# Stick-breaking attention: the last group's first eight row blocks in the order 4, 0, 5, 1, 6, 2, 7, 3

## The chip, the core and the metric

The kernel runs on one core of a Trainium2 chip, as one launch. The metric is the device time in microseconds (us); lower is better. The engines are TensorE (PE, with its weight loads as PEld), VectorE (DVE), ScalarE (ACT), GpSimd (POOL) and SyncE (SP), whose queue issues almost all DMA transfers.

## The reference

One transformer layer on x of 2048 x 1024, float32. A combined projection feeds four differential-attention heads and eight stick-breaking heads; their outputs pass through w_out and are added to x, and a SwiGLU feed-forward part follows. The change is in the stick-breaking part, which is strictly causal and works row block by row block:

```python
z = jnp.einsum('bqhd,bkhd->bhqk', qb, k).astype(jnp.float32) * scale
mask = (k_pos[None, :] < q_pos[:, None])[None, None]
log_1mb = jnp.where(mask, jax.nn.log_sigmoid(-z), 0.0)
rem = lax.cumsum(log_1mb, axis=3, reverse=True) - log_1mb
a = jnp.where(mask, jnp.exp(jax.nn.log_sigmoid(z) + rem), 0.0)
return jnp.einsum('bhqk,bkhd->bqhd', a.astype(v.dtype), v)
```

Each of 16 blocks of 128 queries (a row block) needs the keys of all blocks up to its own, so row block i has i + 1 blocks of keys.

## The kernel before

**Stages.** Matmuls run on 16-bit pairs: every float32 operand is split into a high and a low float16 half. The work goes through eight head groups: groups 0 to 3 are one differential head each, groups 4 to 7 are two stick-breaking heads each. Group by group, the 16 input tiles (128 rows each) are projected, and the attention of a group runs while the next group's tiles are projected. In the last group (7) there is no next group: beside its attention run the rest of its own projection, the loading and splitting of w_out (four quarters, `load_wo`) and, from the second half on, the output projection (`out_proj`, line 814) of rows that all groups have finished. The feed-forward part follows.

**A projected tile** (`proj_tile`, 24 matmuls, L325) is copied out of PSUM and split on ScalarE and VectorE (`proj_out`, L360 to L363). The projection has two PSUM tiles (`pj`, named `osc` or `po` when the weight scales and the output projection use them). After four tiles `proj_batch` turns q and k: two transposing DMAs on SyncE's queue (L409), then two copies of q between partition halves (L411). Row blocks 4j to 4j + 3 need tiles 4j to 4j + 3 and the keys of all tiles before.

**Attention of a row block** (`sb_attn`, line 595). `stage_a(i, m, b)` handles row block i, head m of the two, and a piece b of up to 1024 keys. Per 512 keys TensorE makes the scores (L506, and L508 for the mask) in one of four PSUM tiles `sc`; ScalarE takes two sigmoids (L618, L619); VectorE scans the product of (1 - beta) (L621) and multiplies by beta (L622). Row blocks 0 to 7 have a piece of (i + 1) x 128 keys for each head: VectorE's work grows with i. The piece is then split into halves (`split_t`: L89 on ScalarE, L98 on GpSimd) and turned by a DMA (L460, tile `aT`). `stage_b` makes the values (`pv`, L517) `lag` pieces later (five in the last group). In the last group two row blocks i and i + 1 share a PSUM tile `yp`, and after the second one `finish` normalises, turns and stores them (L475 to L496).

**The order.** The loop at line 647 takes the row blocks 0 to 15 in turn. It yields the share of the group's work that is done, by which the driver (lines 862 to 868) calls for projected tiles, and sets `G["fin"]`, up to which row the output projection may go. The order on each engine is then made by a scheduler when the program is built; on the chip each engine's queue runs in that order.

Of the kernel before, what the change touches and what calls it, by code (L numbers as in the profile page):

```python
# [22 lines left out]
NT, KT, NC = S // P, D // P, S // 512  # L23
# [7 lines left out]
NG = 8  # L31
# [3 lines left out]
LAG0, LAG, PF, CD, CS, LO = 0, 8, 8, 1.0, 1.0, 0.5  # L35
# [24 lines left out]
def block(tc, a, out):  # L60
# [3 lines left out]
    with top:  # L64
# [8 lines left out]
        def note(e, ns):  # L73
            load[e] += ns * KW[e]
# [25 lines left out]
        def pri(k):  # L100
            def deco(f):
                @functools.wraps(f)
                def g(*args):
                    with tc.high_priority(PRI[k]) if PRI[k] else nullcontext():
                        return f(*args)
                return g
            return deco

        def nm(s):
            uid[0] += 1  # L110
            return f"{s}{uid[0]}"
# [144 lines left out]
        with ExitStack() as ph1:  # L256
# [6 lines left out]
            def z4():  # L263
                return zp.tile([P, 1028], F32, tag="z4", bufs=ZB, name=nm("z4"))
# [64 lines left out]
            def turned(g):  # L329
                return 4 <= g < NG - 1  # L330
# [117 lines left out]
            @pri("spl")  # L448
            def split_t(src, n, he="ADP", le="DP", wide=None):
                if wide is not None and wide % 5 in (1, 3):  # L450
                    s16 = pp.tile([P, 4, 256], F32, tag="raw", name=nm("s16"))[:].rearrange("p t n -> p (t n)").bitcast(F16)
                else:
                    s16 = s16p.tile([P, 2048], F16, tag="s16", bufs=SB, name=nm("s16"))
                to16(s16[:, :n], src, n, he)
                tt(s16[:, n : 2 * n], src, s16[:, :n], ALU.subtract, n, le)
                if wide is not None and wide % 4 == 3:
                    aT = pp.tile([P, 4, 4, 2, 64], F16, tag="st", name=nm("aT"))[:].rearrange("p c t s e -> p (c t) (s e)")
                else:
                    aT = sp.tile([P, 16, P], F16, tag="aT", bufs=AB, name=nm("aT"))
                SP.dma_start_transpose(aT[:, : 2 * n // P, :], s16[:, : 2 * n])  # L460
                return aT

            @pri("fin")
            def finish(g, G, i, k, yp, ssum=None):
# [30 lines left out]
                note("D", 350 * k + 200)  # L495
                SP.dma_start(ms[i - k + 1 : i + 1, :, g, :].rearrange("i p n -> p i n"), mo[:, :k].rearrange("p i s n -> p i (s n)"))  # L496

            def fq(g, i):
                k = 2 if g == NG - 1 else 4
                return (i % k, k)  # L500

            @pri("sc")
            def score_chunk(G, sc, i, q, m, w, cut=False, turned=False):
                terms = ((m, 0), (2 + m, 0), (m, 1)) if turned else ((2 + m, m), (m, m))
                for o, (a_, b_) in enumerate(terms):
                    last = PE.matmul(sc[:, : 128 * w].rearrange("p (t n) -> p t n", n=P), lhsT=G["q"][i // 4][:, a_, i % 4, :], rhs=G["k"][q][:, b_, 0:w, :], start=o == 0, stop=o == len(terms) - 1)  # L506
                if cut:
                    last = PE.matmul(sc[:, 128 * w - P : 128 * w], lhsT=idb[:], rhs=tri[:], start=False, stop=True, skip_group_check=True)  # L508
                return last.ins

            @pri("pv")
            def pv(G, yp, y0, aT, b, n, o, wd, start, stop):
                nb = n // P
                for j in range(nb):
                    v = G["v"][2 * b + j // 4][:, j % 4, :]
                    for q, (a_, v_) in enumerate(((j, o), (j, o + wd), (nb + j, o))):
                        PE.matmul(yp[:, y0 : y0 + wd], lhsT=aT[:, a_, :], rhs=v[:, v_ : v_ + wd], start=start and j == 0 and q == 0, stop=stop and j == nb - 1 and q == 2, skip_group_check=True)  # L517
# [77 lines left out]
            def sb_attn(g, G):  # L595
                last = {}
                front = []
                wide = [0]
                lag = PD + 2 if g < NG - 2 else PD

                @pri("at")
                def stage_a(i, m, b):
                    L = (i + 1) * 128
                    n = min(1024, L - 1024 * b)
                    be, om = z4(), z4()
                    if b == i // 8:
                        DVE.memset(om[:, n : n + 1], 8192.0)
                    else:
                        DVE.tensor_copy(om[:, n : n + 1], last[m][:, 0:1])
                    last[m] = om  # L610
                    for c in range((n - 1) // 512, -1, -1):
                        lo, hi = 512 * c, min(512 * c + 512, n)
                        w = hi - lo
                        sc = ps.tile([P, 512], F32, tag="sc", bufs=4, name=nm("sc"))
                        front.append(score_chunk(G, sc, i, 2 * b + c, m, w // P, b == i // 8 and hi == n, turned(g)))
                        aside = c == 1 and turned(g)
                        beta = be[:, lo:hi] if aside else sc[:, :w]
                        ACT.activation(om[:, lo:hi], sc[:, :w], AF.Sigmoid, scale=G["nkz"][:])  # L618
                        ACT.activation(beta, sc[:, :w], AF.Sigmoid, scale=G["kz"][:])  # L619
                        ov = om[:, lo:hi][:, ::-1]  # L620
                        DVE.tensor_tensor_scan(ov, ov, sc[:, :w], om[:, hi : hi + 1], op0=ALU.mult, op1=ALU.bypass)  # L621
                        (POOL if aside else DVE).tensor_tensor(be[:, lo:hi], beta, om[:, lo + 1 : hi + 1], ALU.mult)  # L622
                        note("A", 1.7 * w + 400)
                        note("D", 2.1 * w + 150)
                        note("P" if aside else "D", (1.65 if aside else 1.05) * w + 100)
                    wide[0] += 1
                    return n, split_t(be[:, :n], n, "A", "P", wide[0] if g < NG - 2 else None)

                ypd = {}

                def stage_b(i, m, b, n, aT):
                    with tc.issue_after(front[-1]):
                        stage_c(i, m, b, n, aT)

                def stage_c(i, m, b, n, aT):
                    r, k = fq(g, i)
                    if i // k not in ypd:
                        ypd[i // k] = ps.tile([P, 512], F32, tag="yp", name=nm("yp"))
                    yp = ypd[i // k]
                    pv(G, yp, P * r + 64 * m, aT, b, n, 128 * m, 64, r == 0 and m == 0 and b == i // 8, r == k - 1 and m == 1 and b == 0)  # L640
                    if m == 1 and b == 0 and r == k - 1:
                        finish(g, G, i, k, yp)
                        G["fin"] = i + 1

                pend = []
                done = 0
                for i in range(NT):
                    if i % 4 == 0:
                        level()
                    for b in range(i // 8, -1, -1):  # L650
                        for m in range(2):
                            n, aT = stage_a(i, m, b)
                            pend.append((i, m, b, n, aT))
                            if len(pend) > lag:
                                stage_b(*pend.pop(0))
                            done += n // P + CS
                            yield done / (272 + 48 * CS), (i + 1 if b == 0 and m == 1 else i)
                for u in pend:
                    stage_b(*u)

# [117 lines left out]
            def advance(n):  # L778
                while emitted[0] < min(n, NG * NT):
                    next(stream)  # L780
                    emitted[0] += 1
                if emitted[0] == NG * NT and len(wos) < 4:
                    for _ in stream:
                        pass
                    load_wo(3)
# [74 lines left out]
            outs = 0  # L860
            advance(NT - LAG0)
            for g in range(NG):
                advance(NT * g + 4)
                for fr, i in (diff_attn if g < 4 else sb_attn)(g, Gs[g]):
                    advance(max(NT * g + min(4 * (i // 4 + 1), NT), int(NT * (g + 1 + fr) - (LAG * (1 - LF * fr * (g == NG - 1)) if g else LAG0 + (LAG - LAG0) * fr))))
                    while g == NG - 1 and len(wos) == 4 and outs < Gs[g].get("fin", 0) and (outs + 2) * (outs + 3) / 272 < fr - LO:
                        next(op)
                        outs += 1
# [429 lines left out]
```

## Time and profile before

| | |
|---|---|
| median of 3 runs | 2704.64 us (2703.09 to 2706.77) |
| the profiled execution, own time | 2702.93 us |
| its span, first to last instruction | 2701.0 us |
| TensorE busy | 2508.6 us (93%) |
| VectorE busy | 1959.8 us (73%) |
| ScalarE, GpSimd busy | 1344.7 us (50%), 1517.8 us (56%) |

Times in the profile are in us from the first instruction. A row of the order of time has the start, the duration, the engine, the line and operation, output and inputs by the program's names, the shape, the count of like instructions, and in brackets how long the engine was idle before and what ended that. A row of a group has busy time and mean ns of one instruction behind the first bar, and the idle time ahead of them behind the second. A row of stretches has, for each engine, busy time and instructions, then the granted TensorE clock as a share of full speed, the DMA engines' share and GB/s. In a row of waits stand the total in us, the number of waits and the longest.

### The profile page before, as it was taken

Reading aid. Unit: us, or ns where it says so; the run is one execution under the profiler, and the core shown is the slowest. Engines: PE = TensorE matmul, PEld = TensorE weight load, DVE = VectorE, ACT = ScalarE, POOL = GpSimd, SP = SyncE. Lnnn points to the kernel's source line nnn. Section 1 sums busy time; section 2 is a strip of 40 time slices with the busy share of each in tenths; the row PEclk is TensorE's granted clock in tenths of the full one; section 3 lists DMA queues with packets and bytes.
Section 4 is the critical chain, followed back from the end, with each engine's and each line's share of the span. In section 5 each row is a group of like instructions: output and inputs, shape, how many; then the busy total and the mean of one; then the engine's idle time right before and its main releaser. Section 6 shows DMA issues by size and latency. Waiting matters only on the chain. (4 is left out here: it accounts for less than half of the span.)

```text
span 2701.0 us, 50505 instructions
## 1 busy us (share of the span) xinstructions
PE 2508.6 (93%) x19628; PEld 1507.6 (56%) x19628; DVE 1959.8 (73%) x3712; ACT 1344.7 (50%) x2487; POOL 1517.8 (56%) x1097
## 2 busy tenths in 40 slices
PE   7998989899988989889999999999999999999999
PEld 4655656577776776567774444444444444444444
DVE  6898879899989889887866877778685543433434
ACT  4665656567978878765634534435352112111121
POOL 2578767768767767545665755665564332322323
PEclk9999999999999999999999999999999999999999
DMA  6778697768989989997996566565748744635532
GB/s 221 211 163 184 143 200 172 172 145 183 195 175 185 178 166 206 208 205 203 230 317 232 211 232 219 207 239 183 253 171 330 304 159 157 234 132 184 202 110 94
DMA packets 619584, 534.40 MB, mean 198 GB/s; under 512 B 480640, under 2 KB 548224, under 8 KB 609104
## 3 DMA queue, kind: packets, MB, share of 16 engines
q1 hardware_dynamic: 617520, 529.09, 70.1%
q8 instruction: 154, 2.52, 0.4%
q0 software_dynamic: 512, 1.36, 0.2%
q14 instruction: 86, 0.70, 0.1%
q10 hardware_dynamic: 1312, 0.72, 0.1%
HBM read 261.08 MB, written 147.32 MB: 151 GB/s over the span
## 5 line engine op out<-in xcount | busy, mean ns | idle before, releaser
L98 POOL TENSOR_TENSOR s<-z,s 128x1024 f16<-128x1024 f32 (+7 forms) x288 | 471.5, 1646 | 141.8 <-ACT s L89 118.2
L506 PE MATMUL sc<-kT,qT 128*128 128x512 f16 (+3 forms) x1520 | 382.7, 354 | 51.1 <-DVE z L622 18.6
L1104 PE MATMUL pd<-wd,act 128*128 128x512 f16 x1764 | 392.8, 380 | 5.3 <-DVE cu L1038 4.7
L621 DVE TENSOR_TENSOR_SCAN z<-z,sc 128x512 f32<-128x512 f32 (+3 forms) x320 | 352.8, 1112 | 56.5 <-ACT sc L619 34.6
L325 PE MATMUL pj<-w,xt 128*128 128x384 f16 x1920 | 354.6, 333 | 17.1 <-ACT raw L374 5.8
L1004 PEld LDWEIGHTS <-wu 128*128 128x128 f16 x1848 | 181.9, 98 | 224.6 <-issue 12.8
L1004 PEld LDWEIGHTS <-wg 128*128 128x128 f16 x1848 | 181.3, 98 | 222.9 <-issue 9.3
L517 PE MATMUL yp<-v,aT 128*128 128x64 f16 (+1 forms) x4896 | 271.2, 205 | 36.9 <-DMA aT<-s 35.7
L517 PEld LDWEIGHTS <-aT 128*128 128x128 f16 x4896 | 239.1, 100 | 114.4 <-DMA aT<-s 46.7
L98 POOL TENSOR_TENSOR act<-cg,act 128x512 f16<-128x512 f32 x109 | 150.7, 1393 | 259.4 <-ACT act L1063 259.4
L1104 PEld LDWEIGHTS <-act 128*128 128x128 f16 x1764 | 172.9, 98 | 213.5 <-issue 7.2
L325 PEld LDWEIGHTS <-xt 128*128 128x128 f16 x1920 | 187.8, 99 | 147.2 <-issue 23.4
L89 ACT CAST s<-z 128x128 f16<-128x128 f32 (+7 forms) x215 | 173.3, 810 | 135.9 <-DMA aT<-s 44.6
L98 POOL TENSOR_TENSOR stages<-stages 128x512 f32<-128x512 f32 x97 | 171.4, 1767 | 116.5 <-DVE wg L220 42.2
L618 ACT ACTIVATE z<-sc,c 128x512 f32<-128x512 f32 (+3 forms) x320 | 211.2, 665 | 24.4 <-PE sc L506 12.4
L98 POOL TENSOR_TENSOR hs<-hs,cu 128x512 f32<-128x512 f32 x102 | 133.6, 1317 | 159.3 <-DVE hs L1110 59.7
L506 PEld LDWEIGHTS <-qT 128*128 128x128 f16 x1520 | 128.8, 99 | 119.7 <-issue 23.9
L831 PE MATMUL po<-wo,mt 128*128 128x256 f16 x1536 | 182.4, 279 | 12.6 <-DVE xf L834 8.6
L1063 ACT CAST act<-cg 128x512 f16<-128x512 f32 x126 | 76.7, 616 | 231.1 <-DVE cg L1069 192.7
L1110 DVE SCALAR_TENSOR_TENSOR hs<-pd,c,hs 128x512 f32<-128x512 f32 x144 | 106.0, 747 | 115.0 <-PE pd L1104 105.3
L341 PE MATMUL pj<-xt,w 128*128 128x128 f16 x2304 | 177.4, 222 | 6.2 <-DVE v L363 5.2
L1004 PE MATMUL pm<-X,wu 128*128 128x512 f16 x792 | 179.8, 381 | 2.1 <-ACT cg L1049 1.7
(254 smaller groups left out, 4812.3 us busy)
## 6 DMA issues: line engine op xcount, KB each, us to landing
xt<-xs SPq DMA_DIRECT2D x112, 512.0 KB, 4.5
hs<-hd SPq DMA_DIRECT2D x72, 512.0 KB, 4.5
hd<-hs SPq DMA_DIRECT2D x56, 512.0 KB, 5.9
split<-wg SPq DMA_DIRECT2D x11, 1792.0 KB, 6.9
split<-wu SPq DMA_DIRECT2D x11, 1792.0 KB, 6.7
split<-wd SPq DMA_DIRECT2D x11, 1792.0 KB, 6.8
wg<-split SPq DMA_DIRECT2D x11, 1792.0 KB, 7.5
wd<-split SPq DMA_DIRECT2D x11, 1792.0 KB, 9.0
```

The source lines that it names most:

```text
L89: ACT.copy(dst, src)
L98: (DVE if e == "D" else POOL).tensor_tensor(dst, a_, b_, op)
L325: PE.matmul(pj[:, :384], lhsT=xv[:, xi, kt, :], rhs=G["w"][:, wi, kt, :], start=n == 0, stop=n == 23)
L341: PE.matmul(o, lhsT=x_ if c == 2 else w_, rhs=w_ if c == 2 else x_, start=n == 0, stop=n == 23)
L506: last = PE.matmul(sc[:, : 128 * w].rearrange("p (t n) -> p t n", n=P), lhsT=G["q"][i // 4][:, a_, i % 4, :], rhs=G["k"][q][:, b_, 0:w, :] ...
L517: PE.matmul(yp[:, y0 : y0 + wd], lhsT=aT[:, a_, :], rhs=v[:, v_ : v_ + wd], start=start and j == 0 and q == 0, stop=stop and j == nb - 1 a ...
L618: ACT.activation(om[:, lo:hi], sc[:, :w], AF.Sigmoid, scale=G["nkz"][:])
L621: DVE.tensor_tensor_scan(ov, ov, sc[:, :w], om[:, hi : hi + 1], op0=ALU.mult, op1=ALU.bypass)
L831: PE.matmul(po[:, sl], lhsT=mt[:, kt, P * xi : P * xi + P], rhs=wos[2 * h + n][wi][:, kt, :], start=q == 0, stop=q == 23)
L1004: PE.matmul(ps_[:].rearrange("p (t n) -> p t n", n=P), lhsT=wv[:, wo, wi, 128 * kt : 128 * kt + 128], rhs=X[xo][:, :, xi, kt, :], start=st ...
L1104: PE.matmul(po[:], lhsT=act[:, ao, xi, 128 * j : 128 * j + 128], rhs=W["d"][:, wo, wi, :], start=start and u == 0 and q == 0, stop=u == nu ...
L1110: DVE.scalar_tensor_tensor(dst, po[:], kd[:], src, op0=ALU.mult, op1=ALU.add)
```

## The change

In the last group the first eight row blocks are taken in the order 4, 0, 5, 1, 6, 2, 7, 3; row blocks 8 to 15 and all other groups stay as they were. The bookkeeping follows: a pair of row blocks is finished when its second one is (4 and 5 first, then 0 and 1), `G["fin"]` becomes the first row block that has not ended, and the tiles asked of the projection are those of the highest row block up to the next one.

```diff
+            def row_order(g):
+                pairs = [i for j in range(4) for i in (4 + j, j)]
+                return (pairs if g == NG - 1 else list(range(8))) + list(range(8, NT))
...
                     if m == 1 and b == 0 and r == k - 1:
                         finish(g, G, i, k, yp)
-                        G["fin"] = i + 1
+                        ended.update(range(i - k + 1, i + 1))
+                        G["fin"] = next(t for t in range(NT + 1) if t not in ended)
 
                 pend = []
                 done = 0
-                for i in range(NT):
-                    if i % 4 == 0:
+                ended = set()
+                order = row_order(g)
+                for at, i in enumerate(order):
+                    if at % 4 == 0:
                         level()
...
-                            yield done / (272 + 48 * CS), (i + 1 if b == 0 and m == 1 else i)
+                            yield done / (272 + 48 * CS), (max(order[: at + 2]) if b == 0 and m == 1 else max(order[: at + 1]))
...
-                advance(NT * g + 4)
+                advance(NT * g + 4 * (row_order(g)[0] // 4 + 1))
```

The same instructions stand on each engine in both kernels (one copy of a projected tile moves from VectorE to ScalarE). Their order differs from the place of row block 0's first score on to about row block 12, and in a few swaps at the start of the feed-forward part.

SyncE's queue before, from the last transposes of group 6 on (the first two rows). `aT` of sizes 2, 4, 6 and 8 are row blocks 0, 1, 2 and 3, `aT` of size 10 row block 4; `qT_17777` and `kT_17778` are tiles 4 to 7:

```order
L460 DMA_TRANSPOSE aT_17675<-s_17672 128x16x128
L460 DMA_TRANSPOSE aT_17720<-s_17717 128x16x128
L460 DMA_TRANSPOSE aT_17960<-s_17957 128x2x128
L423 DMA xt_18194<-xs 128x2048
L460 DMA_TRANSPOSE aT_17976<-s_17973 128x2x128
L460 DMA_TRANSPOSE aT_17992<-s_17989 128x4x128
L460 DMA_TRANSPOSE aT_18008<-s_18005 128x4x128
L409 DMA_TRANSPOSE qT_17777<-st_17338 128x8x128
L460 DMA_TRANSPOSE aT_18057<-s_18054 128x6x128
L460 DMA_TRANSPOSE aT_18073<-s_18070 128x6x128
L409 DMA_TRANSPOSE kT_17778<-st_17338 128x8x128
L460 DMA_TRANSPOSE aT_18093<-s_18090 128x8x128
```

The same place on SyncE's queue in the changed kernel (the four `xt` are the inputs of tiles 10 to 13):

```order
L460 DMA_TRANSPOSE aT_17675<-s_17672 128x16x128
L460 DMA_TRANSPOSE aT_17720<-s_17717 128x16x128
L409 DMA_TRANSPOSE qT_17777<-st_17338 128x8x128
L409 DMA_TRANSPOSE kT_17778<-st_17338 128x8x128
L411 DMA qT_17777<-qT_17777 64x1024 x2
L423 DMA xt_18150<-xs 128x2048
L423 DMA xt_18286<-xs 128x2048
L423 DMA xt_18364<-xs 128x2048
L423 DMA xt_18467<-xs 128x2048
L496 DMA ms<-mo_17942 128x4x256
L460 DMA_TRANSPOSE aT_17967<-s_17964 128x10x128
L460 DMA_TRANSPOSE aT_17990<-s_17987 128x10x128
```

The turning of tiles 4 to 7 has moved ahead of every transpose of the group's row blocks, and the first of these is now row block 4's.

ScalarE before, around row block 8's first sigmoid (`z_18717<-sc_18719`). `pj_18474` and `pj_18544` are tiles 13 and 14:

```order
L360 ACTIVATE st_18393<-pj_18474 128x4x64
L89 CAST s_18629<-z_18611 128x1024
L360 ACTIVATE v_18392<-pj_18544 128x2x64
L360 ACTIVATE st_18393<-pj_18544 128x4x64
L618 ACTIVATE z_18717<-sc_18719,c_15239 128x128
L619 ACTIVATE sc_18719<-sc_18719,c_15238 128x128
```

ScalarE in the changed kernel, from row block 3's last sigmoids (`sc_18721`) to row block 8's first (`sc_18747`). `pj_18656` is tile 15, and L189 squares the last quarter of w_out for its scale:

```order
L622 ACTIVATE z_18719<-sc_18721,c_15239 128x512
L623 ACTIVATE sc_18721<-sc_18721,c_15238 128x512
L360 ACTIVATE v_18366<-pj_18656 128x2x64
L189 ACTIVATE wo_18691,m_18701<-z_18692 128x1024
L622 ACTIVATE z_18745<-sc_18747,c_15239 128x128
L623 ACTIVATE sc_18747<-sc_18747,c_15238 128x128
L360 ACTIVATE st_18367<-pj_18656 128x4x64
L189 ACTIVATE wo_18691,m_18701<-z_18693 128x1024
```

Tile 15's first copy and one square have moved ahead of row block 8's first sigmoid. (The changed kernel's line numbers are higher by 4 to 7 behind the new function.)

## The prediction

> **What bounds the kernel now.** I read the page first, then a table of stretches around the changed rows, then TensorE's waits there, then the order of time on each engine.
>
> ```profile
> PE 2508.6 (93%) x19628; PEld 1507.6 (56%) x19628; DVE 1959.8 (73%) x3712; ACT 1344.7 (50%) x2487; POOL 1517.8 (56%) x1097
> core 0: us, PE busy (x) PEld busy (x) DVE busy (x) ACT busy (x) POOL busy (x), PEclk, DMA share, GB/s
> 1086.00:1112.00 26.00, 21.78 (x268) 14.61 (x266) 24.60 (x48) 17.39 (x36) 18.96 (x14) 1.00 0.92 215
> 1112.00:1125.00 13.00, 9.97 (x68) 6.25 (x69) 6.80 (x17) 4.40 (x11) 5.37 (x5) 0.98 0.85 161
> 1125.00:1159.00 34.00, 26.83 (x222) 16.45 (x221) 32.42 (x61) 27.14 (x55) 16.20 (x11) 0.86 0.93 216
> 1159.00:1178.00 19.00, 14.87 (x181) 9.86 (x180) 12.28 (x27) 13.84 (x32) 5.91 (x5) 0.94 1.00 253
> 1178.00:1241.00 63.00, 58.12 (x590) 48.50 (x588) 47.85 (x81) 34.54 (x61) 36.58 (x29) 0.96 0.74 180
> ```
>
> Over the whole span TensorE is the bound. Around the change it isn't. The eight row blocks run from 1086 to 1159, in two halves. Row blocks 0 to 3 end with a lull (1112 to 1125: VectorE busy 6.80 of 13). Row blocks 4 to 7 are VectorE's stage (32.42 of 34.0, 95%). Then a second lull (1159 to 1178: VectorE 12.28 of 19) before row block 8 and the first out-projection. From 1178 TensorE is busy 58.12 of 63, so a lead on TensorE there is a lead of the kernel. In the first four stretches (92 us) TensorE is idle 18.6 us: the most that a better order could find.
>
> ```profile
> PE sc L506 <- DVE z L622: 5.1, 7, 2.1
> PE pj L325 <- DVE st L363: 3.5, 3, 1.9
> PE sc L506 <- DMA qT<-qT: 2.7, 1, 2.7
> ```
>
> These are TensorE's largest waits from 1086 to 1178: on scans, on copies that free the projection's two PSUM tiles, and once on the turned q of tiles 4 to 7, which row block 4 needs.
>
> **The change part by part.** It removes and adds no work. It takes row block 4 first, so nothing of the eight can start until tiles 4 to 7 are projected and turned.
>
> *Row block 4 starts earlier, 0 to 3 later.*
>
> ```profile
> 1088.41 4.07 PE L325 MATMUL pj<-w,xt 128*128 128x384 f16 x24
> 1094.36 0.97 PE L325 MATMUL pj<-w,xt 128*128 128x384 f16 x5
> 1097.72 1.95 PE L325 MATMUL pj<-w,xt 128*128 128x384 f16 x11 [0.46 <-DVE st L363]
> 1103.26 4.23 PE L325 MATMUL pj<-w,xt 128*128 128x384 f16 x25
> 1107.32 1.65 PE L517 MATMUL yp<-v,aT 128*128 128x64 f16 x51
> 1124.25 0.22 PE L506 MATMUL sc<-kT,qT 128*128 128x128 f16 x1 [2.69 <-DMA qT<-qT]
> 1097.15 0.42 DVE L363 SCALAR_TENSOR_TENSOR st<-pj,st 128x256 f16<-128x256 f32 x1
> 1112.57 1.26 SPq L409 DMA_TRANSPOSE qT<-st  x1
> 1116.57 1.31 SPq L409 DMA_TRANSPOSE kT<-st  x1
> 1121.15 1.20 SPq L411 DMA_DIRECT2D qT<-qT  x2
> ```
>
> With the scores of rows 0 to 3 gone from this place, TensorE ends tile 6 at about 1093 and has nothing until tile 5's copy frees a PSUM tile. That copy ends at 1097.57 now, and some 0.5 earlier without row 0's scan and product ahead of it: tile 7 starts at 1097.1, after 4.1 us of idle. Ahead of row 4's first score then stand three tiles of 24 matmuls (0.163 each by the 4.07 row: 3.9 a tile), 96 value matmuls of row block 15 (51 took 1.65: 2.8), and 0.5 for a weight scale: 15.0 us. The clock adds something: both halved stretches below follow idle time.
>
> ```profile
> 1124.50:1134.70 10.20, 7.50 (x57) 4.41 (x55) 9.09 (x18) 9.59 (x22) 3.82 (x3) 0.50 0.91 302
> 1175.70:1182.50 6.80, 5.97 (x30) 3.91 (x30) 3.71 (x15) 5.56 (x12) 6.47 (x5) 0.50 0.74 169
> ```
>
> In the second, half of 5.97 busy us was lost, 3.0; so the gap costs 0 to 3.0, and I take 1.7. Row 4's scores come at 1097.1 + 15.0 + 1.7 = 1114, against 1124.25. The turns don't bind: before, four transposes of rows 2 and 3 stood among those of tiles 4 to 7 on SyncE's queue; now the three issues follow each other from about 1106, and the copies' 3.1 us (1121.15 to 1124.25) end near 1113. Behind them on SyncE the loads of tiles 10 to 13 stand ahead of row 4's first transpose, and the last of these must wait for tile 10's matmuls, about 1121 (1114, row 4's 1.6 of scores, 3.9, and 1.5 of other matmuls between). Row 4's halves are split at about that time too, and five later pieces run before its values are wanted: I cost this at 0, and 1 us if that cover is gone.
>
> On a gap like this one the Trainium skill ("TensorE: Matmul & The Clock Gate", "HAM oscillation — how this bites in real kernels") warns of idle gaps over about 3.4 us. The trace is stricter: the clock halved at 1124.5 behind a wait of 2.69, and at 1175.7 behind waits of at most 1.47. By the page only the new 4.1-us gap would be punished and the sum stays at -4; by the trace short gaps ahead of the out-projection can be too, and it would be about -1.
>
> *One run of eight row blocks instead of two halves.*
>
> ```profile
> L621 DVE TENSOR_TENSOR_SCAN z<-z,sc 128x512 f32<-128x512 f32 x10 | 12.7, 1274 | 0.4 <-ACT sc L619 0.3
> L622 DVE TENSOR_TENSOR z<-sc,z 128x512 f32<-128x512 f32 x10 | 6.8, 681 | 0.2
> L621 DVE TENSOR_TENSOR_SCAN z<-z,sc 128x384 f32<-128x384 f32 x2 | 2.0, 1002 | 0.0
> L621 DVE TENSOR_TENSOR_SCAN z<-z,sc 128x256 f32<-128x256 f32 x2 | 1.5, 728 | 0.0
> L622 DVE TENSOR_TENSOR z<-sc,z 128x384 f32<-128x384 f32 x2 | 1.1, 552 | 0.1
> L621 DVE TENSOR_TENSOR_SCAN z<-z,sc 128x128 f32<-128x128 f32 x2 | 0.9, 474 | 2.7 <-ACT sc L619 2.7
> L622 DVE TENSOR_TENSOR z<-sc,z 128x256 f32<-128x256 f32 x2 | 0.8, 418 | 0.0
> L622 DVE TENSOR_TENSOR z<-sc,z 128x128 f32<-128x128 f32 x2 | 0.6, 284 | 0.0
> 1125.19 0.48 DVE L621 TENSOR_TENSOR_SCAN z<-z,sc 128x128 f32<-128x128 f32 x1 [2.66 <-ACT sc L619]
> 1158.70 0.06 DVE L607 MEMSET z<- 128x1 f32 x1
> 1165.33 0.48 DVE L621 TENSOR_TENSOR_SCAN z<-z,sc 128x128 f32<-128x128 f32 x1 [2.47 <-ACT sc L619]
> ```
>
> Scan and product cost 0.76, 1.15, 1.55 and 1.96 for blocks of 128 to 512, twice (two heads) a row: rows 0 to 3 are 2 x 5.42 = 10.8 us. Before, that lay in the time in which tiles 4 to 7 were waited for; now it stands in the run. Rows 4 to 7 took 33.5 (1125.19 to 1158.70). Add 10.8, and 2.0 for a few copies (0.42 each) and the end of group 6's last output that fall into the run now: 46.3. From row 4's first scan (1114 + 0.9) the run would end at 1161.2. What I charge beyond that are two places in ScalarE's order.
>
> ```profile
> 1124.60 1.25 SPq L802 DMA_DIRECT2D z<-in_w_out_dram  x2
> 1132.96 1.05 ACT L189 ACTIVATE wo<-z 128x1024 bf16<-128x1024 f32 x1
> 1164.70 0.37 ACT L618 ACTIVATE z<-sc,c 128x128 f32<-128x128 f32 x1 [2.29 <-PE sc L506]
> ```
>
> First, the square of the third quarter of w_out. It ran 8.4 us after its loads were issued. The loads now come behind three transposes of rows 4 and 0, at about 1127, so the square comes near 1135.5, while row 6's sigmoids, which stand behind it, could run at about 1133.5: 2 us. Second, tile 15's copy and another square now stand ahead of row 8's first sigmoid (before, only tile 14's copies did). From row 3's last score TensorE has tiles 14 and 15 (7.8), some 105 value matmuls (3.1) and row 8's own scores (1.0, and a short wait for a free tile): about 13 us. VectorE has about 10.5 left there. With the square (1.05) this costs 4 us. Row 8's first scan comes at 1161.2 + 2 + 4 = 1167 to 1168, against 1165.33: VectorE is 2.5 late.
>
> *The out-projection starts earlier.*
>
> ```profile
> 1174.68 0.60 PE L506 MATMUL sc<-kT,qT 128*128 128x512 f16 x2 [1.47 <-DVE z L607]
> 1177.84 6.48 PE L831 MATMUL po<-wo,mt 128*128 128x256 f16 x37
> 1241.01 0.28 PE L506 MATMUL sc<-kT,qT 128*128 128x128 f16 x2
> ```
>
> Its first matmul stood behind row block 9's first scores, which wait for scans (1.47 at 1174.68). Now it stands behind row 8's only and the last weight scale, whose second square follows row 8's first sigmoid by about 2 us: 1170. Some 3.3 us of scores and values that were done before it now come later. TensorE's lead is 1177.84 - 1170 - 3.3 = 4.5. To row block 12's first score (1241.01) it has about the same matmuls left in both kernels and is busy 92% of the time, so the lead holds; for VectorE's 2.5 I take off 0.5. From there the engines' orders agree, but for a few swaps where the feed-forward part starts, which I cost at 0 (1 either way).
>
> **Sum:** -4 us. The profiled execution took 2702.93 (span 2701.0 and 1.9 around it), so 2698.9 of it; the median of the runs is 2704.64, 1.7 above, so I say 2700.6.
>
> **Rivals.** A measurement of this kernel can tell about 0.2% (5.4 us) from no change.
>
> *VectorE is late and passes it on (slower).* In the mixed run large and small blocks alternate, and VectorE waits for ScalarE at small ones: the 128 blocks' rows show 2.7 us of idle before two scans, the 512 blocks' 0.4 before ten. Against it: the 2.7 is row 4's start. If VectorE packs the run to 80% instead of 95%, 46.3 becomes 55, row 8's scan comes at about 1176, and the first out-projection at 1178.5: with the 3.3 that is +4 on TensorE, and with VectorE 11 late the scores between the out-projection's matmuls make TensorE wait: +8, 2712.6. It decides from row 8's first scan at about 1171.
>
> *The lulls really go (clearly faster).* No wait in ScalarE's order: row 8 at 1161.2, the out-projection at 1164, and the halved stretch at 1175.7 (3.0) gone with the waits ahead of it. TensorE's lead would be 1177.84 - 1164 - 3.3 = 10.5; I give 9, since VectorE would be only 4 early: 2695.6. For it speaks that TensorE is no obstacle beside the run (26.83 of 34.0 busy); against it stand the two places in ScalarE's order. That the change doesn't reach the engines at all is out: their order shows it.
>
> **How the numbers follow.** Forecast 0.48 (-8 to 0 around -4), clearly faster 0.20, slower 0.32. Of the forecast three tenths lie beyond -5.4, of the slower case three quarters beyond +5.4. Faster: 0.48 x 0.3 + 0.19 = 0.33; slower 0.24, say 0.25; the rest, 0.42, within 0.2%. The range of 8 in 10 takes most of both rivals: 2691 to 2712.
>
> **What would show it.** Row 4's first score near 1114 behind one TensorE gap of about 4 us; VectorE above 90% busy from there to row 3's scans; row 8's first scan at 1165 to 1169; the first out-projection by 1171; row block 12's first score near 1237. A first scan of row 8 behind 1171, or an out-projection that starts early and then waits for its PSUM tiles, would prove me wrong.

## The result and the profile after

The changed kernel is slower: its median is 2713.36 us (17 runs, 2706.53 to 2729.47) against 2705.57 (17 runs, 2700.83 to 2712.96) for the kernel before on the same chip, a ratio of 1.0031 with a 95% interval of 1.0018 to 1.0044. That is 8.4 us more (4.9 to 11.9), where 4 less were forecast, and outside the range.

The page of the changed kernel, its span and the engines' busy time:

```profile
span 2711.4 us, 50503 instructions
...
PE 2503.5 (92%) x19628; PEld 1502.0 (55%) x19628; DVE 1960.6 (72%) x3711; ACT 1345.0 (50%) x2488; POOL 1517.3 (56%) x1097
```

The span is 10.4 us longer and TensorE is busy 5.1 us less: over the whole program all the loss is idle time. The stretches that the prediction used, for the changed kernel:

```profile
core 0: us, PE busy (x) PEld busy (x) DVE busy (x) ACT busy (x) POOL busy (x), PEclk, DMA share, GB/s
1086.00:1112.00 26.00, 21.73 (x207) 13.85 (x206) 17.20 (x33) 7.36 (x15) 14.68 (x9) 0.93 1.06 237
1112.00:1125.00 13.00, 8.17 (x63) 4.90 (x62) 11.46 (x27) 11.30 (x28) 3.52 (x4) 0.87 0.68 161
1125.00:1159.00 34.00, 30.02 (x269) 18.87 (x268) 30.49 (x63) 27.78 (x57) 20.22 (x16) 0.95 0.81 200
1159.00:1178.00 19.00, 12.89 (x136) 8.99 (x135) 9.62 (x25) 9.41 (x24) 5.12 (x6) 0.82 0.99 231
1178.00:1241.00 63.00, 52.46 (x542) 42.77 (x541) 49.84 (x82) 38.47 (x68) 35.00 (x26) 0.95 0.72 177
```

VectorE's lull of 1112 to 1125 is gone (11.46 of 13 busy, 6.80 before). But TensorE's idle time of the first four stretches is 19.2 us (92 less 72.81), not less than the 18.6 of before: it only lies elsewhere. And from 1178 to 1241, where TensorE was to keep its lead, it is busy 52.46 of 63 instead of 58.12.

To see where the time goes over the whole program, each TensorE instruction was matched with the same one in the profile of before; the table has the median difference of their starts in four stretches (us, times of before; positive is later):

| | 1000-1080, ahead of the change | 1390-1440, behind the attention | 1640-1720, in the feed-forward part | 2400-2680, near the end |
|---|---|---|---|---|
| changed kernel | -2.6 | 2.9 | 9.9 | 10.3 |
| changed kernel, profiled again | -0.2 | 2.3 | 9.3 | 9.0 |

So there are two steps. The attention moves by +5.5 in one execution and +2.5 in the other; the start of the feed-forward part adds 7.0 in both. Behind it nothing more is lost. The prediction had -4 and 0 for them. The 7.0 stands out from the spread of single executions; the attention's step hardly does: five kernels of the experiments below, whose attention is that of before, have steps from -0.1 to +4.0 there, 2.4 on average.

**The start of the feed-forward part.** Each kernel's TensorE waits from 1440 to 1560, of before and then of after (`xtr` are transposes of the rows that have just been normalised, `pa` the first products of the feed-forward part):

```profile
PE xtr L1178 <- DVE bx L228: 3.4, 2, 3.1
...
PE pa L1004 <- ACT cg L1014: 1.7, 1, 1.7
```

```profile
PE xtr L1185 <- DVE bx L228: 7.8, 2, 6.9
PE pa L1011 <- ACT cg L1021: 4.1, 2, 2.4
```

These two waits have grown most, by 4.4 and 2.4 us. They are not the whole of the 7.0: the same matmuls take 235.06 us before (1425.13 to 1660.19) and 242.00 after (1428.00 to 1670.00), in which TensorE is busy 215.75 and 218.65 at a mean granted clock of 0.98 and 0.96. So its idle time grows by 4.0, since other waits became shorter, and its busy time by 2.9. Both waits lead back to ScalarE, but to two places in its queue. The first place: ScalarE's order of time before, with the row of SyncE that loads row 14 (`bx`, the second of two such loads; the longer of their two landings took 9.7 us by the view of that line):

```profile
1474.96 2.55 SPq L1169 DMA_DIRECT2D bx<-hd  x1
```

```profile
1476.50 2.19 ACT L215 ACTIVATE wu<-stages,c 128x1024 f16<-128x1024 f32 x2 [0.25 <-DVE c L204]
...
1479.21 0.56 ACT L1014 COPY cg<-pa 128x512 f32<-128x512 f32 x1
1482.90 1.91 ACT L937 ACTIVATE sq<-stages 128x2048 bf16<-128x2048 f32 x1 [3.13 <-DMA stages<-in_w_gate_dram]
...
1485.23 1.05 ACT L225 ACTIVATE bx<-bx 128x1024 f32<-128x1024 f32 x1
```

And ScalarE in the changed kernel at the same place:

```profile
1482.01 1.06 ACT L225 ACTIVATE bx<-bx 128x1024 f32<-128x1024 f32 x1 [3.59 <-DMA bx<-hd]
...
1483.07 2.17 ACT L215 ACTIVATE wu<-stages,c 128x1024 f16<-128x1024 f32 x2
...
1485.76 1.04 ACT L225 ACTIVATE bx<-bx 128x1024 f32<-128x1024 f32 x1
...
1486.80 0.56 ACT L1021 COPY cg<-pa 128x512 f32<-128x512 f32 x1
```

L225 is the square that normalises a row. Before, both squares (rows 14 and 15) stood behind the scaling of w_up (L215) and behind the copy that frees TensorE's PSUM tile (`cg<-pa`). Now the first stands ahead of the scaling and the second ahead of the copy. The square's row is not there yet: ScalarE idles 3.59 us with ready work behind the square, and the copy runs at 1486.80 instead of 1479.21. (It is row 14 that is late. Row 15, loaded first, had landed 4.6 us after its issue at 1469.90.) TensorE does not wait for that copy in this execution; the chain goes from the square to VectorE and back to TensorE (VectorE's row, then TensorE's):

```profile
1483.19 0.15 DVE L155 TENSOR_SCALAR xrs<-xss 128x1 f32<-128x1 f32 x1 [4.01 <-ACT bx L225]
```

```profile
1500.95 1.73 PE L1185 MATMUL xtr<-id,bx 128*128 128x128 f32 x7 [6.89 <-DVE bx L228]
```

VectorE, in order too, idles 4.01 for the square's sum, and TensorE 6.89 for the normalised row. By the matched starts TensorE is 3.6 us late from 1480 to 1490 (times of before) and 6.9 from 1490 to 1500: 3.3 of the 7.0 arise here.

The second place lies 50 us further on, where w_down is scaled. ScalarE in the changed kernel, and TensorE's wait behind it:

```profile
1534.12 0.62 ACT L1070 CAST act<-cg 128x512 f16<-128x512 f32 x1 [4.41 <-DVE cg L1076]
...
1535.70 0.56 ACT L1021 COPY cg<-pa 128x512 f32<-128x512 f32 x1
```

```profile
1536.31 2.75 PE L1011 MATMUL pa<-X,wg 128*128 128x512 f16 x12 [2.37 <-ACT cg L1021]
```

Here a copy of a product (`act<-cg`) has moved ahead of a scaling of w_down and of another PSUM copy, and ScalarE idles 4.41 for VectorE's product. Before, the scaling ran at 1522.85, the PSUM copy at 1523.90 and the product's copy behind both at 1525.62, and TensorE did not wait for that PSUM copy. From 1510 to 1560 the matched starts go from 6.9 to 9.8 us late (7.5 to 9.6 when profiled again).

**The attention.** TensorE's order of time in the changed kernel, the rows that answer to the prediction's:

```profile
1094.43 5.01 PE L325 MATMUL pj<-w,xt 128*128 128x384 f16 x20 [4.27 <-DVE st L363]
...
1111.05 0.82 PE L510 MATMUL sc<-kT,qT 128*128 128x128 f16 x6
...
1171.81 4.93 PE L838 MATMUL po<-wo,mt 128*128 128x256 f16 x24 [2.90 <-DMA mt<-ms]
...
1225.07 5.71 PE L838 MATMUL po<-wo,mt 128*128 128x256 f16 x26 [5.75 <-DVE xf L841]
...
1246.57 0.27 PE L510 MATMUL sc<-kT,qT 128*128 128x128 f16 x2
```

By these rows the first out-projection (`po`) starts 6.0 us earlier than before (1177.84), but row block 12's first score comes 5.6 later (1241.01 before). (The whole profile is 2.6 early ahead of the change; without that it is 3.4 earlier and 8.2 later.) In between lies one wait of 5.75 for VectorE's sums, the largest of four with 8.7 in all from 1178 to 1241, where before there were three with 3.3 and none over 1.3. Output row 2 is added to its x only when that x is there, and its x goes into the tile of row 0's x, which is free when row 0 has been normalised. On VectorE in the changed kernel:

```profile
1214.83 2.17 DVE L228 SCALAR_TENSOR_TENSOR z<-xf,xrs,bias 128x1024 f32<-128x1024 f32 x1 [0.97 <-POOL xrs L156]
...
1224.54 0.88 DVE L841 SCALAR_TENSOR_TENSOR xf<-po,c,xf 128x256 f32<-128x256 f32 x2 [0.94 <-DMA xf<-in_x_dram]
```

and the load of that x on SyncE's queue, before and then after:

```profile
1217.18 0.42 SPq L823 DMA_DIRECT2D xf<-in_x_dram  x1
```

```profile
1220.07 8.27 SPq L830 DMA_DIRECT2D xf<-in_x_dram  x2
```

Row 0's normalisation starts at 1214.07 in the kernel before, 0.8 earlier, though row 0's sums are ready 9 us later there. The earlier out-projection filled its two PSUM tiles and then stood still.

### The profile page after: what moved, and what is told of

Its sections match the earlier page's. It is cut to its first block, busy times and chain, and to the rows that moved or that the text cites. A ratio compares the mean times of both kernels' runs of the same rounds, so it can differ in the third digit from the quotient of the medians.

```text
span 2711.4 us, 50503 instructions
## 1 busy us (share of the span) xinstructions
PE 2503.5 (92%) x19628; PEld 1502.0 (55%) x19628; DVE 1960.6 (72%) x3711; ACT 1345.0 (50%) x2488; POOL 1517.3 (56%) x1097
## 5 line engine op out<-in xcount | busy, mean ns | idle before, releaser
L1111 PEld LDWEIGHTS <-act 128*128 128x128 f16 x1764 | 172.8, 98 | 216.9 <-issue 10.4
L838 PE MATMUL po<-wo,mt 128*128 128x256 f16 x1536 | 184.2, 279 | 19.8 <-DVE xf L841 13.1
```

What stands on the lines that cost most here:

```text
L838: PE.matmul(po[:, sl], lhsT=mt[:, kt, P * xi : P * xi + P], rhs=wos[2 * h + n][wi][:, kt, :], start=q == 0, stop=q == 23)
L1111: PE.matmul(po[:], lhsT=act[:, ao, xi, 128 * j : 128 * j + 128], rhs=W["d"][:, wo, wi, :], start=start and u == 0 and q == 0, stop=u == nu ...
```

## The experiments

Two theories. **Late square:** most of the loss comes from the start of the feed-forward part, from ScalarE's queue there. **Lost lead:** it comes from the attention, where VectorE or the out-projection's waits eat the lead, and the later difference only follows. In the names of the runs, a stands for the changed kernel and b for the kernel before. All were timed against the kernel before on the same chip; a result is the median in us, its ratio to that kernel, and in brackets the ratio's 95% interval.

### Which of the two places

The start of the feed-forward part is pinned: each engine's instructions there get order edges, which fix their order in the queue and add no wait, in the order that they have in the other kernel. All else stays in its order. The pins cost nothing that the runs show: two kernels pinned in the same way, b_sp_after and b_pe_after below, are at 0.9995 and 0.9998.

```diff
+FFN_ORDER = {
+    'PE': [(843, 845), (804, 815), ...],
+    'DVE': [...], 'Activation': [...], 'Pool': [...], 'SP': [...],
+}
...
+            for runs in FFN_ORDER.values():
+                seq = [f"I-{first + n}" for lo, hi in runs for n in range(lo, hi + 1)]
+                for u, v in zip(seq, seq[1:]):
+                    tc.add_manual_dep(traced[v], u, mybir.DependencyInfo(mybir.DependencyClass.NoSync, ...
```

The new attention with the old start of the feed-forward part:

> The changed kernel, its row order and all of its attention as it is, but the start of the feed-forward part queued on every engine in the order of the kernel before. Theory 1 (two losses: about 5 to 7 us where the feed-forward part starts, the rest in the attention): 2706 to 2708, so 1.000 to 1.001 of the kernel before, and TensorE busy about 110 of the 120 us after 1440 again. Rival 2 (the loss is all in the attention, and the feed-forward part's waits would come anyway): stays at about 2713, 1.003. Rival 3 (the attention costs nothing, all of the loss is the feed-forward order): 2705, 1.000 with the same times as before at row block 12's first score.

Measured: 2705.82, 1.0008 (0.9996 to 1.0019). The old attention with the new start:

> The kernel before, with its row order 0 to 7 and all of its attention, but the start of the feed-forward part queued on every engine in the order that the changed kernel has there. Theory 1: the 5 to 7 us come over, 2711 to 2713, 1.002 to 1.003. Rival 2: no change, 2705 to 2706. Rival 3: the whole loss comes over, 2713 to 2714.

Measured: 2714.82, 1.0043 (1.0027 to 1.0060). The whole loss comes with the start of the feed-forward part, without one row block being moved; and the new row order by itself is within 0.2%. The theory of the lost lead falls as the main cause. But the new attention doesn't bring the -4 either.

### Which engine's queue

The same pins, in the kernel before, with the list of one engine, or of three, from the changed kernel:

```diff
-    'Activation': [..., (869, 869), (916, 916), (922, 922), (926, 926), (955, 955), (1004, 1004), (892, 892), (930, 930), ...],
+    'Activation': [..., (869, 869), (930, 930), (916, 916), (922, 922), (926, 926), (936, 936), (955, 955), (1004, 1004), (892, 892), ...],
```

Here 930 and 936 are the squares of rows 14 and 15, 916, 922 and 926 the scaling of w_up, and 955 the copy `cg<-pa`. The lists differ in a few more places: an earlier PSUM copy stands behind two other copies, and around 1530 lies the second place of above.

ScalarE's list alone, SyncE's alone, TensorE's alone, and the lists of ScalarE, VectorE and GpSimd together:

> The kernel before, all queues as before, but ScalarE's queue at the start of the feed-forward part in the order of the changed kernel (the two squares of rows 14 and 15 ahead of the scaling of w_up). Theory 1 (the squares on ScalarE make most of the feed-forward loss): 1.002 to 1.004 of the kernel before, and 4 us or more between 1440 and 1640. Rival (it takes the other queues too): 1.000 to 1.0015.

> The kernel before, but SyncE's queue at the start of the feed-forward part in the order of the changed kernel (the load of the next w_gate piece behind a store that waits for its data and behind the load of row 14). Theory 1: 1.000 to 1.001. Rival (the late load of w_gate makes the loss): 1.002 to 1.004.

> The kernel before, but TensorE's queue at the start of the feed-forward part in the order of the changed kernel (some groups of matmuls swapped). Theory 1: 1.000 to 1.001, 0 to 2 us between 1440 and 1640. Rival (TensorE's own order makes the loss): 1.002 to 1.004.

> The kernel before, but ScalarE's, VectorE's and GpSimd's queues at the start of the feed-forward part in the order of the changed kernel; TensorE's and SyncE's as before. Theory 1 (ScalarE's squares carry it, VectorE's order only follows them): as with ScalarE's queue alone, 1.002 to 1.004. Rival (VectorE's order adds its own waits): 0.001 or more above ScalarE's alone.

Measured: ScalarE alone 2713.61, 1.0046 (1.0033 to 1.0059); SyncE alone 2699.18, 0.9995 (0.9983 to 1.0007); TensorE alone 2701.51, 0.9998 (0.9983 to 1.0012); the three engines 2714.39, 1.0044 (1.0030 to 1.0059). ScalarE's order alone has the whole loss, 12.4 us of 2703. Its rows in that run, ScalarE first, then TensorE:

```profile
1482.95 1.06 ACT L234 ACTIVATE bx<-bx 128x1024 f32<-128x1024 f32 x1 [7.74 <-DMA bx<-hd]
...
1484.00 2.17 ACT L224 ACTIVATE wu<-stages,c 128x1024 f16<-128x1024 f32 x2
...
1487.73 0.56 ACT L1023 COPY cg<-pa 128x512 f32<-128x512 f32 x1
```

```profile
1488.34 4.14 PE L1013 MATMUL pa<-X,wg 128*128 128x512 f16 x12 [6.94 <-ACT cg L1023]
```

This is the first place of the changed kernel, and larger: the square idles 7.74 for its row, and TensorE waits 6.94 directly for the copy behind it. By the matched starts this run is 0.8 us early from 1470 to 1480 and 7.7 late from 1480 to 1490. So 8.5 of its step of 10.3 arise at this copy, and the other swaps of the list add little: at the earlier PSUM copy nothing is lost that lasts (0.1 late from 1440 to 1450, 0.8 early from 1470 to 1480), and at the second place it stays 7.8 and 7.7 late.

The other way round, the changed kernel with the queues of ScalarE, VectorE and GpSimd at that place as before (TensorE's and SyncE's as changed), beside the changed kernel itself on the same chip:

> The changed kernel with ScalarE's, VectorE's and GpSimd's queues at the start of the feed-forward part as before; TensorE's and SyncE's there as changed. Theory 1 (ScalarE's queue makes the loss): 0.9995 to 1.002 of the kernel before, what is left being the attention's share, and ScalarE waits less than 1 us for row 14. Rival: 1.003 or above, as the changed kernel.

> The changed kernel itself on the same chip, to hold beside the other two. Every theory: 1.002 to 1.0055 of the kernel before, with ScalarE waiting 2 to 5 us for row 14.

Measured: 2707.41, 1.0013 (1.0001 to 1.0024), and 2712.59, 1.0047 (1.0028 to 1.0065). TensorE's waits from 1440 to 1560 with the three queues put back:

```profile
PE xtr L1194 <- DVE bx L237: 3.5, 3, 1.8
...
PE pa L1020 <- ACT cg L1030: 1.7, 1, 1.7
```

These are the values of before again (3.4 and 1.7). With the matched starts of the table, the step from 1390-1440 to 1640-1720 is, kernel by kernel:

| ScalarE's order there | step, us |
|---|---|
| as changed: the changed kernel twice, b_ffn_after, b_act_after, b_elem_after | 7.0, 7.0, 6.1, 10.3, 13.1 |
| as before: a_ffn_before, a_elem_before, b_sp_after, b_pe_after | -1.6, 0.5, 1.3, 2.0 |

### The squares alone

In the changed kernel, the normalisation is issued behind the scaling of w_up:

```diff
+                    scaled = [k for k in nc.cur_bb.bb.instructions if k.engine == mybir.EngineType.Activation][-1]
...
-                        norm_tile(z[:], z[:], w2f[:], xt[:])
+                        with tc.issue_after(scaled) if j == 3 else nullcontext():
+                            norm_tile(z[:], z[:], w2f[:], xt[:])
```

> The changed kernel with one thing different in the feed-forward part: on ScalarE the two squares that normalise rows 14 and 15 are queued behind the scaling of the second w_up piece, as they stood before; every other order is left to the scheduler. Theory 1 (these two squares, which wait for rows that come late from DRAM, hold the scaling and VectorE behind them, and make nearly all of the feed-forward loss): 1.000 to 1.0015 of the kernel before, and TensorE's wait of 6.9 us ahead of the second transposes of that part falls to 3 us or less. Rival (other swaps there, on VectorE, GpSimd or TensorE, matter as much): 1.002 to 1.003.

Measured: 2710.56 (2702.14 to 2723.28), 1.0042 (1.0026 to 1.0058): not the 1.000 to 1.0015 of its theory. The profiled execution was the fastest of its twelve, 2702.14, and in it the step at the start of the feed-forward part is 2.2 us instead of 7.0:

```profile
1472.41 2.19 ACT L215 ACTIVATE wu<-stages,c 128x1024 f16<-128x1024 f32 x2 [0.25 <-DVE c L204]
...
1475.98 1.06 ACT L225 ACTIVATE bx<-bx 128x1024 f32<-128x1024 f32 x1 [0.77 <-DMA bx<-hd]
...
1477.04 0.57 ACT L1021 COPY cg<-pa 128x512 f32<-128x512 f32 x1
```

With three instructions ahead of it, the square idles 0.77 instead of 3.59. But the timed runs did not come down, so its profile settles little. The edit is no test of the two squares alone either. The first square still stands ahead of the copy `cg<-pa`, and a load that lands later would hold the copy again; the second place is as in the changed kernel (ScalarE idles 4.41 for `act<-cg`, TensorE 1.68 for the copy behind it); and the scheduler, to which the other orders were left, gave the other engines new orders there too. No profile shows which of these costs the slower executions their time. So that the loss comes through ScalarE's queue is shown; how much of it the squares carry is read from the waits and the matched starts (8.5 of 10.3 in b_act_after, 3.3 of 7.0 in the changed kernel), and this run does not confirm it.

### Why the attention brings nothing

First, the wait for the x of rows 2 and 3: they get tiles of their own, with the start of the feed-forward part pinned to the order of before; the same for the kernel before:

```diff
-                    spare[13 if n == 0 else 14] = t16[:, 4096:6144]
+                    spare[13 if n == 0 else 14] = spare[2 if n == 0 else 3] = t16[:, 4096:6144]
```

> As the first kernel of this call (changed row order, feed-forward order of before), and the x rows of output rows 2 and 3 are loaded into tiles of their own, free since the weights were split, in place of the two tiles that rows 0 and 1 use. Theory 1 (the out-projection's lead is lost because row 2's x waits until row 0 is normalised): the wait of 5.75 us ahead of row 2's second half goes, row block 12's first score comes 4 us or more earlier than in the first kernel, and the time is 2 to 4 us less than the first kernel's. Rival (VectorE and ScalarE set the pace of row blocks 9 to 12, so the wait only moves): row block 12's first score within 1.5 us of the first kernel's, and the same time within 1.5 us.

> The kernel before (row order 0 to 7, its own feed-forward order) with the x rows of output rows 2 and 3 in tiles of their own. Theory 1: before, the out-projection waits for row 2's x only 1.3 us, so it gains 0 to 2 us: 2703.5 to 2705.5. Rival (the two shared tiles bound both kernels alike): 4 us less, 2701 to 2702.

Measured: 2709.16, 1.0029 (1.0015 to 1.0042) for the new row order, and 2699.59, 0.9993 (0.9981 to 1.0005) for the old. The first is 3.3 us slower than a_ffn_before on the same chip, where the theory had 2 to 4 less. In it the wait at 1225 is gone, but not the waits for VectorE's sums, which now come later, the longest here:

```profile
1289.36 4.96 PE L847 MATMUL po<-wo,mt 128*128 128x256 f16 x31 [6.23 <-DVE xf L850]
```

From 1165 to 1300 they are 13.9 us in all, against 11.5 in a_ffn_before and 7.4 in the kernel before. A start of the out-projection that is early only finds the next thing that isn't ready. Second, the first output row's matmuls are held back in a_ffn_before until row block 9's last score:

```diff
+                        if g == NG - 1 and i == 9:
+                            hold[:] = front[-1:]
...
+                                  with tc.issue_after(hold[0]) if t == 0 else nullcontext():
                                     PE.matmul(po[:, sl], ...
```

> The changed row order with the feed-forward order of before, and the output projection's first row held on TensorE behind row block 9's last scores, where it stood before. Theory 1 (the early start is worth nothing, since rows 2 and 3 wait for VectorE and ScalarE anyway, and it costs a halved clock): the same time as without it or up to 3 us less, 0.9995 to 1.001 of the kernel before, the wait of 5.4 us ahead of row 2's second half shorter, and TensorE no later at 1290 to 1370. Rival (the lead is worth what it looks like): 3 to 5 us more, 1.002 or above.

Measured: 2708.18, 1.0022 (1.0007 to 1.0038). The number is the rival's (1.002 or above), but the interval holds both theories. TensorE's waits for the out-projection's tiles from 1165 to 1300 are less than half of a_ffn_before's 11.5, with no gain in the time:

```profile
PE po L850 <- DVE xf L853: 4.5, 5, 2.7
```

Third, two milder orders that interleave less, with the old start of the feed-forward part:

```diff
-                pairs = [i for j in range(4) for i in (4 + j, j)]
+                pairs = [0, 4, 1, 5, 2, 6, 3, 7]
```

> Row order 0, 4, 1, 5, 2, 6, 3, 7 with the feed-forward order of before: one small row block ahead of row block 4. Theory 1 (the attention loses because small row blocks that used to fill the wait for tiles 4 to 7 now stand in VectorE's run, and because TensorE idles 4.3 us in their place): between the kernel before and the changed order, 1.000 to 1.001, TensorE's gap ahead of tile 7 below 3 us, and VectorE about 1.5 us earlier at row block 8. Rival (the loss comes from the early out-projection alone, whatever row comes first): as with row block 4 first, about 4 us late at 1290 to 1370.

and `[0, 1, 4, 2, 5, 3, 6, 7]`:

> Row order 0, 1, 4, 2, 5, 3, 6, 7 with the feed-forward order of before: two small row blocks ahead of row block 4. Theory 1: nearer still to the kernel before, 0.9995 to 1.0005, VectorE 2 to 4 us earlier at row block 8 than with row block 4 first. Rival: as with row block 4 first.

Measured: 2703.61, 1.0018 (1.0001 to 1.0035), and 2706.85, 1.0026 (1.0010 to 1.0042). Neither is better than a_ffn_before, so no order of this kind among those tried beats the kernel before. The theory that the milder order comes nearer to the kernel before is not borne out: the second is above the 0.9995 to 1.0005 that it gave.

Fourth, the place in ScalarE's order that the prediction charged with 4 us: in a_ffn_before, row block 8's first four sigmoids go ahead of tile 15's copies and of the last two squares of w_out. Theory 1 says that VectorE then gains at row 8, and the kernel with it.

```diff
+    'row 8': [(-3122, -3122), (-3097, -3097), (-3096, -3096), (-3072, -3072), (-3071, -3071), (-3167, -3167), (-3146, -3146), (-3165, -3165), (-3145, -3145)],
```

> The changed row order with the feed-forward order of before, and on ScalarE row block 8's first four sigmoids ahead of tile 15's copies and the last squares of w_out. Theory 1 (this place in ScalarE's order delays VectorE and is what the attention loses): VectorE's gap of 3 us ahead of row block 8 goes, its first scan comes 3 us earlier, and the time is 2 to 4 us less than with the feed-forward order alone, 0.9985 to 1.0005 of the kernel before. Rival (early or late at row block 8 is evened out by the out-projection's rows 1 to 3, which wait for other things): within 1.5 us of the feed-forward order alone, 1.0005 to 1.002.

Measured: 2716.31, 1.0055 (1.0037 to 1.0073): slower than both theories had it, and than a_ffn_before (1.0008). VectorE's row 8 did come earlier, by 3.5 us when the 3.8 that a_ffn_before's profile is early ahead of the change are taken off. Its two first scans, with row 3's last one ahead of them, in a_ffn_before and then in this run:

```profile
1157.68 1.28 DVE L634 TENSOR_TENSOR_SCAN z<-z,sc 128x512 f32<-128x512 f32 x1 [0.58 <-ACT sc L632]
1163.61 0.48 DVE L634 TENSOR_TENSOR_SCAN z<-z,sc 128x128 f32<-128x128 f32 x1 [0.63 <-ACT sc L632]
1168.32 0.48 DVE L634 TENSOR_TENSOR_SCAN z<-z,sc 128x128 f32<-128x128 f32 x1
```

```profile
1161.73 1.28 DVE L635 TENSOR_TENSOR_SCAN z<-z,sc 128x512 f32<-128x512 f32 x1 [0.58 <-ACT sc L633]
1163.86 0.48 DVE L635 TENSOR_TENSOR_SCAN z<-z,sc 128x128 f32<-128x128 f32 x1
1164.99 0.48 DVE L635 TENSOR_TENSOR_SCAN z<-z,sc 128x128 f32<-128x128 f32 x1 [0.25 <-ACT sc L633]
```

From row 3's last scan to row 8's second head it is 3.3 us instead of 10.6. But TensorE then stood at values whose pieces were not turned yet:

```profile
1176.47 0.82 PE L531 MATMUL yp<-v,aT 128*128 128x64 f16 x12 [5.12 <-DMA aT<-s]
```

Such waits are 7.8 us from 1165 to 1300, and 0.5 in a_ffn_before. The place was worth something to VectorE, and the kernel got slower. This run and a_out_late don't show the price of their edits alone, though: the scheduler made a new order for the rest of the attention in both, on TensorE and SyncE too.

## Why the prediction was wrong, step by step

The rows of the changed kernel's profile are 2.6 us early ahead of the change, so 2.6 is added to its times here.

- **Row block 4's first score at 1114, behind one gap of 4.1: right.** It came at 1113.6 (1111.05), behind a gap of 4.27. The 1.7 for the clock was right as well: tile 7's 20 matmuls took 5.01 where 20 at the 0.170 of before take 3.4. Its 0.163 a matmul is not 4.07 for 24 (0.170), as the step says, but the distance of two rows' starts: 25 matmuls from 1103.26 to 1107.32.
- **VectorE's run of 46.3: right.** From row 4's first scan to the end of row 3's it is 47.5 us, 90% busy:

```profile
1112.79 0.48 DVE L625 TENSOR_TENSOR_SCAN z<-z,sc 128x128 f32<-128x128 f32 x1
...
1159.06 1.28 DVE L625 TENSOR_TENSOR_SCAN z<-z,sc 128x512 f32<-128x512 f32 x1 [0.58 <-ACT sc L623]
...
1164.98 0.48 DVE L625 TENSOR_TENSOR_SCAN z<-z,sc 128x128 f32<-128x128 f32 x1 [0.63 <-ACT sc L623]
```

- **Row 8's first scan at 1167 to 1168: right**, at 1167.6 (1164.98). Of the two places in ScalarE's order, the second held: ScalarE waited 4.12 us for tile 15 at 1163.15. The first did not: the square ahead of row 6's sigmoids ran at 1131.4 (1128.80), 4.6 us after its loads were issued and without a wait, not near 1135.5. So the sum came out with some luck: this place cost nothing where 2 was charged, but the run came out 1.2 longer and the second place 0.6 dearer.
- **The first out-projection at 1170: 4.4 late**, at 1174.4 (1171.81). TensorE waited three times ahead of it that the step did not list: 1.40 and 1.80 for the weight scale's squares, which waited 1.97 for their load, and 2.90 for the turned rows (`mt`). With the 3.3 of work that now comes later, the step's lead is 0.1 in place of 4.5.
- **"To row block 12's first score ... the lead holds": wrong.** It came at 1249.2 (1246.57), where 1237 was forecast and 1241.01 measured before; the largest wait on the way is the 5.75 at 1225. It had been named as what would prove the prediction wrong, "an out-projection that starts early and then waits for its PSUM tiles", but no case had a price for it: 92% busy TensorE was taken as a sign that time won at its start would be kept, while the sums that free its tiles are tied to loads and normalisations that had not moved. Of the 8.2 us, 2.7 come back by 1390 to 1440. In place of -4 the attention alone gives +2 to +3.5 us by the two timed kernels with ScalarE's old order at the feed-forward start (1.0008 and 1.0013; by their intervals -1 to +6.5). That the 4 us are not gained is shown; that the attention loses is not clear of the spread.
- **"From there the engines' orders agree, but for a few swaps where the feed-forward part starts, which I cost at 0 (1 either way)": this step failed most.** The swaps cost 7.0 us in both profiles of the changed kernel, and ScalarE's alone +12.4 by time (+8.9 to +15.9) in the kernel before. Zero had no reason beside it, and the size could be read from before's rows: the scaling ran at 1476.50, the copy at 1479.21 and the square only at 1485.23, half a us after its row had landed (issued at 1474.96, 9.7 to land). To put the square ahead of the first two is to put it ahead of work that was ready 8.7 and 6.0 us before the square ran.

The rival that ended on the right side (VectorE late) was not what happened: its point of decision, row 8's first scan at 1171, was not reached, and that its 2712.6 lies near the measured time is chance. What remains open: the attention's share between -1 and +6.5; which executions of a_norm_late lose what; how the changed kernel's 7.0 divide between the two places in its slower executions; and why row 14's load takes 8.6 to 10.8 us to land, kernel by kernel, when the load of row 15, issued just ahead of it, takes 4.5 to 6.2.

## What to carry to other kernels

Price every swap in an engine's queue, also those far behind the place of the change: an instruction that moves ahead of ready work costs that engine the time until its input lands, and the rows of the kernel before already show both times. A lead on the busiest engine was gone here at the next things that were not ready, so follow each thing that the early work needs (the tile, its load, what frees it) before it is carried to the end. Where a change is spread over two places, a kernel with the one and a kernel with the other, queue by queue, settle in a few runs which of them has the loss.

## What the runs showed of the hardware

The granted clock fell to half behind shorter waits than the prediction's new gap. Stretches of the changed kernel around its first out-projection:

```profile
1162.00:1169.30 7.30, 3.71 (x39) 2.12 (x37) 2.25 (x8) 4.18 (x12) 0.34 (x1) 1.00 0.92 250
1169.40:1171.80 2.40, 0.00 (x0) 0.00 (x0) 2.30 (x11) 2.40 (x6) 1.57 (x3) 0.50 1.57 288
1171.80:1176.60 4.80, 4.79 (x25) 3.47 (x26) 2.50 (x4) 1.91 (x5) 3.11 (x4) 0.54 0.74 162
```

The clock is halved already 0.5 us into the wait of 2.90 that ends at 1171.81. Ahead of that wait stand two others, of 1.40 and 1.80, in 7.30 us of which TensorE was busy 3.71. The Trainium skill ("TensorE: Matmul & The Clock Gate", "HAM oscillation — how this bites in real kernels") puts the limit at gaps of about 3.4 us; in this trace the clock is halved below it.

Executions of one kernel are not alike. The attention's queues of before took up to 4 us more from one profiled execution to another: the matched starts behind the attention, less those ahead of the change, are 2.9, 2.1, 4.0, 3.1 and -0.1 us for five kernels that have the attention's queues as before (b_ffn_after, b_act_after, b_elem_after, b_sp_after, b_pe_after). For the changed attention they are 5.5 and 2.5, and 4.2 and 2.2 in a_ffn_before and a_elem_before. A single pair of profiles can't tell 3 us of an edit from that; the timed intervals and the stretch where the difference arises have to agree.
